# Attention scores computed for two heads at once on the two row halves of the array, in three products of 64 rows

## The chip, the cores and the metric

The kernel runs on one core of a Trainium2 chip. The metric is the device time of one execution in microseconds; lower is better. It is taken several times, and the median counts. Beside the timed runs, one execution is recorded by the hardware profiler, and every row below comes from such a record.

## The reference

The reference is a block of two layers over 512 latent tokens and 256 context tokens of 1024 features. Layer 0 is windowed attention with 16 query heads of 64 features, two key heads and a sink logit for each head. Layer 1 is differential attention with 8 heads, each with two score maps of 64 features. After each attention comes a squared-ReLU MLP. In outline, cut to the scores:

```
# layer 0, per block of 128 queries; keys: the block and its neighbours, and 256 context keys
s_lat = einsum('bqhgd,bkhd->bhgqk', qblk, kblk) * scale      # masked outside the window
s_ctx = einsum('bqhgd,bchd->bhgqc', qblk, kc) * scale
p     = softmax_with_sink(concatenate([s_lat, s_ctx]), sink)
o     = p[latent] @ v + p[context] @ vc
# context queries see the 256 context keys alone

# layer 1, per block of 128 queries; keys: all 768 tokens
s = einsum('bqhtd,bkhtd->bhtqk', qblk, keys) * scale          # t = 0, 1
p = softmax(s);  a = p[:, :, 0] - lam * p[:, :, 1]
o = a @ v_all
```

Everything is in float32.

## The kernel before, in words

**Products in parts.** A float32 operand is split into a high part of type float32r and the rest as a low part, both in SBUF (`split`, L505; `wsplit`, L301). A product of two such operands is three products, high by high, high by low and low by high (`mm3`, L324 to L327). The scores use another form. The head size is 64, so a score product has 64 rows to sum over, and the array has 128. In layer 1 the transposed keys of one map (`kS`) hold the high part in rows 0 to 63 and the low part in rows 64 to 127. The queries are written twice before they are transposed, so `qT` holds the high part in both halves, and, beside it, the low part in both halves. Two products of 128 rows then give all four combinations of parts. In layer 0 the roles are turned: the transposed keys are doubled (`kT[:, kvh, hl]`), and the queries of a head hold the high part above the low part.

**Layer 0.** `group(n, tb, qd)` (L1302) handles one block of 128 queries and four heads: 24 groups, 16 for the four latent blocks and 8 for the two context blocks. For each head it takes a score slot and an `e` tile, issues two products with the latent keys of the window (L1322; 256 or 384 columns) and two with the context keys (L1326; 256 columns). VectorE adds the mask, takes the minimum and copies the scores out of PSUM into `e`, and that frees the score slot. ScalarE takes the exponential, GpSimd scales, TensorE transposes (`pT_ps`, L1377) and multiplies by the values (`o_ps`, L1359, in two column halves of 64).

**Layer 1.** `post1` (L1612) takes a block of a head's projections, applies the rotation, splits keys and queries (`sk`, `sq`) and transposes them: two transposes for the keys (L1642) and, for latent blocks, four for the queries (L1657). `scores1` (L1726) goes over four query blocks, and for each over the two maps `tt`: one score slot, four products of 384 columns (L1738), a minimum on VectorE, an exponential on ScalarE straight from PSUM. The exponential frees the slot. `att1` (L1768) transposes the result and multiplies by the values.

**Score slots.** PSUM has two score tiles of 1024 columns, two banks each (tag "S", `psS`), counted by `sS = Slots(fl, 2)`. `ok` says that at least one is free, `spare` (L197) that at least two are. The `e` tiles are counted in the same way: `eS` in layer 0 (six at first, more later), `eS1` in layer 1 (five).

**What sets the order.** TensorE's order is written out by hand: a planner (`Flow`) runs the jobs as Python generators. A job yields a condition, and the planner takes the first job, by priority, whose condition holds at its own modelled time. The model charges `mm(n)` for a product and `dve`, `act`, `pool2` for the other engines. TensorE then works strictly in the order that came out. In layer 0 the groups have priorities 0.5 to 0.73; the query projections `proj` have 2 and the output projection 3. In layer 1 `att1` has 0.2, `scores1` 0.5, `post1` 1, `proj1` 2 and the output projection `out1` 3. The other engines' order follows the dependencies of the program.

Of the kernel before, what the change touches and what calls it, by code (L numbers as in the profile page):

```python
# [13 lines left out]
F32 = mybir.dt.float32  # L14
# [16 lines left out]
GRID_W = 64  # L31
ROPE_BASE = 10000.0
# [202 lines left out]
def hybrid_block(ctx: ExitStack, tc: tile.TileContext, t: dict, out: bass.AP):  # L235
# [834 lines left out]
    with tc.tile_pool(name="qpool", bufs=6, side="right") as qpool, \  # L1070
# [164 lines left out]
        def q_post(half, tb, pt, p, give):  # L1235
# [9 lines left out]
            stg = stg.rearrange("p (g u d) -> p g u d", g=8, u=2)  # L1245
            _, r = split(512, r, qr, stg[:, :, 0], stg[:, :, 1])
# [7 lines left out]
            for j in range(8):  # L1254
                nc.tensor.transpose(out=pq.bitcast(F32R)[:, j * P:(j + 1) * P], in_=stg[:, j], identity=identr)
# [3 lines left out]
            qT[(half, tb)] = qt.rearrange("p (h t) -> p h t", h=8)  # L1259
# [42 lines left out]
        def group(n, tb, qd):  # L1302
# [9 lines left out]
            for j in range(4):  # L1312
                yield [sS.ok, eS.ok]
                hd_ = qd * 4 + j
                q_ = qT[(kvh, tb)][:, hd_ % 8]
                esl.append(eS.take())
                e = etile(esl[-1])
                sp = psS("s_ps")
                slot = sS.take()
                for hl in range(2):  # L1320
                    if nl:
                        nc.tensor.matmul(out=sp[:, 512 - nl:512], lhsT=q_,  # L1322
                                         rhs=kT[:, kvh, hl, lat[0] * P:lat[0] * P + nl],
                                         start=(hl == 0), stop=(hl == 1))
                for hl in range(2):
                    nc.tensor.matmul(out=sp[:, 512:512 + CTX], lhsT=q_,  # L1326
                                     rhs=kT[:, kvh, hl, SEQ:TOK], start=(hl == 0), stop=(hl == 1))
                p = fl.pe(2 * mm(CTX) + (2 * mm(nl) if nl else 0))
                eo, si = e[:, 0:W_], sp[:, 512 - nl:512 + CTX]
                if tb == NXB - 1:  # L1330
                    mk = mask.rearrange("p (a b) k -> p a b k", a=2)[:, :, 0:2]
                    eo = eo.rearrange("p (a b k) -> p a b k", a=2, b=2)
                    si = si.rearrange("p (a b k) -> p a b k", a=2, b=2)
                else:
                    mk = mask.rearrange("p a b -> p (a b)")[:, 5 * P - W_:5 * P]
                nm = small.tile([P, 1], F32, name="nm", tag="nm")
                d = dv(W_ + 70, [p], nc.vector.tensor_tensor_reduce, out=eo, in0=si, in1=mk, scale=1.0,
                       scalar=nsink[:, hd_:hd_ + 1], op0=ALU.add, op1=ALU.min, accum_out=nm)
                sS.give(slot, d)

                d = [d, ac(1, [], nc.scalar.copy, out=e[:, W_:W_ + 1], in_=nsink[:, hd_:hd_ + 1])]
                sm = small.tile([P, 1], F32, name="sm", tag="sm")
                a = ac(W_ + 200, d, nc.scalar.activation, out=e[:, 0:W_ + 1], in_=e[:, 0:W_ + 1], func=AF.Exp,
                       scale=-1.0, bias=nm, accum_out=sm)
                d = dv(8, [a], nc.vector.reciprocal, out=sm, in_=sm)
                ready.append(gp(W_ * 0.0019 + 0.1, [d], nc.gpsimd.tensor_tensor, lat=ELAT, out=e[:, 0:W_], in0=e[:, 0:W_],
                                in1=sm.broadcast_to([P, W_]), op=ALU.mult))
                es.append(e)
                yield
# [241 lines left out]
    with tc.tile_pool(name="attn1", bufs=1, reuse_waits="tile") as pool:  # L1591
# [20 lines left out]
        def post1(hd_, tb, pt, p, give, R):  # L1612
# [39 lines left out]
            if isx:  # L1652
# [3 lines left out]
                for i in range(4):  # L1656
                    nc.tensor.transpose(out=pq.bitcast(F32R)[:, i * P:(i + 1) * P], in_=sq[:, i // 2, i % 2], identity=identr)  # L1657
# [419 lines left out]
```

## Time and profile before

| what | time |
|---|---|
| median of three runs | 1665.86 us |
| lowest and highest | 1658.1 and 1666.66 us |
| the profiled execution | 1660.59 us |
| its span, first to last instruction | 1658.5 us |
| its mean granted TensorE clock | 0.983 |
| scores of layer 0 on TensorE, first to last start | 74.8 to 298.4 us |
| scores of layer 1 on TensorE, first to last start | 929.8 to 1235.4 us |

In the rows of the profile, PE is TensorE's products and PEld its weight loads, DVE is VectorE, ACT is ScalarE and POOL is GpSimd. A row of the timeline gives a start, a length and how many like instructions were merged. The length of a product includes its way through the array, so successive products overlap in the rows; what a product costs when TensorE is the limit is the distance from its start to the next start. A form such as 128*64 128x256 says that the weights have 128 rows and 64 columns and that 256 columns are streamed.

### The profile page before, as it was taken

To read this page: it belongs to the slowest core of one execution; us is meant where nothing else is said; L and a number is where in the kernel's file an instruction comes from. 1 tells how busy PE (TensorE), PEld (TensorE's weight loads), DVE (VectorE), ACT (ScalarE), POOL (GpSimd) and SP (SyncE) were. 2 spreads that over 40 slices of the span, in tenths; PEclk is the share of its full clock that TensorE was granted. 3 is DMA by queue.
4 is the path that set the end of the run, shared out by engine and by line. 5 is a ranking of instruction groups with operands and counts; after the bars stand their busy time and mean duration, and the time that the engine had idled before them with its cause. 6 is when DMAs were issued, how large, how long until landed. Compare 5 with 4: busy or idle time off the path is not lost.

```text
span 1658.5 us, 25161 instructions
## 1 busy us (share of the span) xinstructions
PE 1572.0 (95%) x9465; PEld 1384.3 (83%) x9465; DVE 1139.5 (69%) x2199; ACT 790.7 (48%) x1683; POOL 440.4 (27%) x369
## 2 busy tenths in 40 slices
PE   7899999989999999999997999999989799999987
PEld 5788777789888998989986999899878789999986
DVE  4655676699776689766466677777765866666677
ACT  3465676364343334335416555555552745555450
POOL 1333444106111121211191222220100112222363
PEclk9999999999999999999998999999999899999998
DMA  9111550533454434443323122211132333333321
GB/s 372 43 52 33 179 178 26 197 128 128 143 162 150 140 103 163 153 141 115 125 71 111 52 70 64 74 46 39 48 115 90 102 115 102 102 102 102 102 77 51
DMA packets 66434, 181.17 MB, mean 109 GB/s; under 512 B 7368, under 2 KB 13320, under 8 KB 66312
## 3 DMA queue, kind: packets, MB, share of 16 engines
q1 hardware_dynamic: 66312, 179.56, 32.1%
q8 instruction: 74, 1.21, 0.3%
q14 instruction: 48, 0.39, 0.1%
HBM read 168.49 MB, written 11.04 MB: 108 GB/s over the span
## 4 chain that ended last, share of the span: by engine, by line
PE 53%; DVE 17%; DMA 11%; issue 7%; ACT 6%; POOL 5%; SPq 0%; DVEq 0%; POOLq 0%; ACTq 0%
PE y_ps L325 6%; PE y_ps L327 6%; PE y_ps L326 6%; DMA w_raw<-in_w_adaT 6%; PE h_ps L325 4%; PE h_ps L326 4%; PE h_ps L327 4%; DVE w_raw L260 2%; DVE w_l L314 2%; PE o_ps L1359 2%; PE pT_ps L1377 2%; PE qkv_ps L325 2%; PE qkv_ps L326 2%; PE qkv_ps L327 2%; PE s_ps L1738 2%
## 5 line engine op out<-in xcount | busy, mean ns | idle before, releaser
L325 PE MATMUL y_ps<-w_h,hid 128*128 128x512 f32 (+1 forms) x648 | 255.5, 394 | 3.3 <-ACT hid L264 2.4
L327 PE MATMUL y_ps<-w_h,hid 128*128 128x512 f32 (+1 forms) x648 | 254.6, 393 | 2.6 <-DVE hid L260 2.6
L326 PE MATMUL y_ps<-w_l,hid 128*128 128x512 f32 (+1 forms) x648 | 254.7, 393 | 0.5 <-DVE w_l L314 0.5
L314 DVE TENSOR_TENSOR w_l<-w_raw,w_h 128x1024 fp32r<-128x1024 f32 (+1 forms) x133 | 158.1, 1199 | 61.7 <-ACT w_h L264 58.5
L264 ACT CAST w_h<-w_raw 128x1024 fp32r<-128x1024 f32 (+1 forms) x133 | 131.2, 1001 | 113.8 <-PE y_ps L327 65.2
L268 POOL TENSOR_TENSOR w_sum<-w_raw 128x512 f32<-128x512 f32 x26 | 55.2, 2121 | 420.7 <-DMA w_raw<-in_w 272.7
L327 PEld LDWEIGHTS y_ps<-w_h,hid 128*128 128x128 f32 x648 | 123.6, 191 | 29.9 <-DVE hid L260 4.1
L325 PEld LDWEIGHTS y_ps<-w_h,hid 128*128 128x128 f32 x648 | 123.7, 191 | 27.1 <-ACT hid L264 3.5
L326 PEld LDWEIGHTS y_ps<-w_l,hid 128*128 128x128 f32 x648 | 123.8, 191 | 22.7 <-DVE w_l L314 0.9
L264 ACT CAST w_half<-w_raw 128x512 fp32r<-128x512 f32 x130 | 80.2, 620 | 114.1 <-PE h_ps L327 69.2
L325 PE MATMUL qkv_ps<-w_h,hx 128*128 128x384 f32 (+1 forms) x384 | 127.9, 333 | 3.4 <-ACT w_h L264 3.3
L260 DVE TENSOR_TENSOR w_half<-w_raw,w_half 128x512 fp32r<-128x512 f32 x130 | 105.9, 822 | 29.8 <-ACT w_half L264 28.1
L326 PE MATMUL qkv_ps<-w_l,hx 128*128 128x384 f32 (+1 forms) x384 | 123.1, 321 | 1.7 <-DVE w_l L314 1.7
L327 PE MATMUL qkv_ps<-w_h,hx 128*128 128x384 f32 (+1 forms) x384 | 122.8, 320 | 0.0
L268 POOL TENSOR_TENSOR e<-e,sm 128x512 f32<-128x512 f32 (+2 forms) x96 | 92.6, 977 | 109.6 <-DVE sm L260 91.0
L260 DVE CUSTOM_DVE_ANT_0 w_raw<-w_raw,cB 128x512 f32<-128x512 f32 x112 | 82.9, 768 | 42.0 <-DMA w_raw<-in_w_adaT 41.8
L260 DVE TENSOR_TENSOR fx<-y_ps,fx 128x512 f32<-128x512 f32 x110 | 75.3, 687 | 39.2 <-PE y_ps L327 38.4
L264 ACT ACTIVATE relu<-relu 128x384 f32<-128x384 f32 (+3 forms) x104 | 69.7, 672 | 50.1 <-DVE relu L260 49.0
L268 POOL TENSOR_TENSOR rope<-rope,rope 128x256 f32<-128x256 f32 (+1 forms) x40 | 33.8, 844 | 221.6 <-DVE rope L260 175.2
L264 ACT COPY relu<-h_ps 128x384 f32<-128x384 f32 (+1 forms) x78 | 32.9, 422 | 119.5 <-PE h_ps L327 113.0
L264 ACT ACTIVATE e<-e,nm 128x513 f32<-128x513 f32 (+2 forms) x96 | 65.9, 688 | 33.1 <-DVE nm L260 26.4
L325 PEld LDWEIGHTS qkv_ps<-w_h,hx 128*128 128x128 f32 x384 | 72.9, 190 | 5.3 <-ACT w_h L264 3.8
(267 smaller groups left out, 4329.6 us busy)
## 6 DMA issues: line engine op xcount, KB each, us to landing
w_raw<-in_w SPq DMA_DIRECT2D x128, 512.0 KB, 3.5
w_raw<-in_w_adaT SPq DMA_DIRECT2D x56, 512.0 KB, 3.8
w_raw<-in_w_ada SPq DMA_DIRECT2D x24, 512.0 KB, 4.3
w_raw<-in_b_w SPq DMA_DIRECT2D x32, 384.0 KB, 3.8
raw<-in_w_ada SPq DMA_DIRECT2D x16, 512.0 KB, 9.6
w_raw<-in_a_wq SPq DMA_DIRECT2D x8, 512.0 KB, 8.0
w_raw<-in_a_wo SPq DMA_DIRECT2D x8, 512.0 KB, 4.3
w_raw<-in_b_wo SPq DMA_DIRECT2D x8, 512.0 KB, 4.5
```

The costliest lines, as they stand in the source:

```text
L260: fn(**kw)
L264: fn(**kw)
L268: fn(**kw)
L314: last["split"] = nc.vector.tensor_tensor(**kw)
L325: nc.tensor.matmul(out=o, lhsT=lh, rhs=rh, start=start, stop=False, **kw)
L326: nc.tensor.matmul(out=o, lhsT=lh, rhs=rl, start=False, stop=False, **kw)
L327: last["pe"] = nc.tensor.matmul(out=o, lhsT=ll, rhs=rh, start=False, stop=stop, **kw)
L1359: nc.tensor.matmul(out=po[odd * HD:odd * HD + HD, 0:256], lhsT=vv[:, kb, kvh], rhs=pt_[:, odd * 256:odd * 256 + 256], start=(i == 0), stop ...
L1377: nc.tensor.transpose(out=pp[:, c * P:(c + 1) * P], in_=es[j][:, i * P:(i + 1) * P], identity=ident)
L1738: nc.tensor.matmul(out=sp[:, c * 512:c * 512 + 384], lhsT=qTt[:, tt, hl, qb * P:(qb + 1) * P], rhs=kS[:, tt, c * 384:c * 384 + 384], start ...
```

## The change

Two heads of layer 0, or the two maps of a head in layer 1, are computed together. One lies in rows 0 to 63 of the transposed tiles, the other in rows 64 to 127. For each stretch of keys there are three passes (`PASSES`): high by high, high by low, low by high. Low by low is no longer computed. In each pass one product of 64 rows is issued for the first head and one for the second, into two different score tiles. So a pair has six products where two heads had four.

- `q_post` (layer 0) stores the split queries as high part, then low part, and transposes two heads at a time: still eight transposes a block.
- `post1` (layer 1) no longer doubles the queries: the split works on half the elements, there are two transposes a block instead of four, and `qT1` is half as large. `sk` is laid out by part first, so that `kS[:, part]` holds the two maps in its two row halves.
- Both score loops take two score slots and two `e` tiles at once; they wait for `spare` where they waited for `ok`. The softmax of both heads is issued after all products of the pair.
- The planner is told three products of each length for a pair.

The core of the diff (the softmax lines of layer 0 are only indented further):

```diff
+PASSES = ((0, 0), (0, 1), (1, 0))
...
-            stg = stg.rearrange("p (g u d) -> p g u d", g=8, u=2)
-            _, r = split(512, r, qr, stg[:, :, 0], stg[:, :, 1])
+            sh, sl = [stg[:, x:x + 512].rearrange("p (g d) -> p g d", d=HD) for x in (0, 512)]
+            _, r = split(512, r, qr, sh, sl)
...
-            qT[(half, tb)] = qt.rearrange("p (h t) -> p h t", h=8)
+            qT[(half, tb)] = qt.rearrange("p (h j t) -> p h j t", h=2, j=4)
...
-            for j in range(4):
-                yield [sS.ok, eS.ok]
...
-                for hl in range(2):
-                    if nl:
-                        nc.tensor.matmul(out=sp[:, 512 - nl:512], lhsT=q_,
-                                         rhs=kT[:, kvh, hl, lat[0] * P:lat[0] * P + nl],
-                                         start=(hl == 0), stop=(hl == 1))
-                for hl in range(2):
-                    nc.tensor.matmul(out=sp[:, 512:512 + CTX], lhsT=q_,
-                                     rhs=kT[:, kvh, hl, SEQ:TOK], start=(hl == 0), stop=(hl == 1))
-                p = fl.pe(2 * mm(CTX) + (2 * mm(nl) if nl else 0))
...
+            for j in range(2):
+                yield [sS.spare, eS.spare]
+                q_ = qT[(kvh, tb)][:, :, (qd % 2) * 2 + j]
+                two = []
+                for i in range(2):
+                    esl.append(eS.take())
+                    two.append((qd * 4 + 2 * j + i, etile(esl[-1]), psS("s_ps"), sS.take()))
+                for o, k0, n in ([(512 - nl, lat[0] * P, nl)] if nl else []) + [(512, SEQ, CTX)]:
+                    for ph, pk in PASSES:
+                        for i in range(2):
+                            r_ = slice(i * HD, i * HD + HD)
+                            nc.tensor.matmul(out=two[i][2][:, o:o + n], lhsT=q_[r_, ph], rhs=kT[r_, kvh, pk, k0:k0 + n],
+                                             start=(ph == 0 and pk == 0), stop=(ph == 1))
+                p = fl.pe(3 * mm(CTX) + (3 * mm(nl) if nl else 0))
+                for hd_, e, sp, slot in two:
...
-            _, d1 = split(P, r, kr, sk[:, :, 0], sk[:, :, 1], [rsk.get()])
+            _, d1 = split(P, r, kr, sk[:, 0], sk[:, 1], [rsk.get()])
             if isx:
-                sq = pool.tile([P, 2, 2, 2, HD], F32R, name="sq", tag="sq", bufs=SB)
-                q_ = qk[:, 0:2].unsqueeze(2).broadcast_to([P, 2, 2, HD])
-                _, d2 = split(256, r, q_, sq[:, :, 0], sq[:, :, 1], [rsq.get()])
+                sq = pool.tile([P, 2, 2, HD], F32R, name="sq", tag="sq", bufs=SB)
+                _, d2 = split(P, r, qk[:, 0:2], sq[:, 0], sq[:, 1], [rsq.get()])
...
-                for i in range(4):
-                    nc.tensor.transpose(out=pq.bitcast(F32R)[:, i * P:(i + 1) * P], in_=sq[:, i // 2, i % 2], identity=identr)
-                p = fl.pe(4 * mm(P))
+                for i in range(2):
+                    nc.tensor.transpose(out=pq.bitcast(F32R)[:, i * P:(i + 1) * P], in_=sq[:, i], identity=identr)
+                p = fl.pe(2 * mm(P))
...
-                for tt in range(2):
-                    yield [sS.ok, eS1.ok]
...
-                    for c in range(2):
-                        for hl in range(2):
-                            nc.tensor.matmul(out=sp[:, c * 512:c * 512 + 384], lhsT=qTt[:, tt, hl, qb * P:(qb + 1) * P],
-                                             rhs=kS[:, tt, c * 384:c * 384 + 384], start=(hl == 0), stop=(hl == 1))
...
+                yield [sS.spare, eS1.spare]
+                two = [(psS("s_ps"), sS.take(), eS1.take()) for _ in range(2)]
+                for c in range(2):
+                    for ph, pk in PASSES:
+                        for tt in range(2):
+                            r_ = slice(tt * HD, tt * HD + HD)
+                            nc.tensor.matmul(out=two[tt][0][:, c * 512:c * 512 + 384],
+                                             lhsT=qTt[r_, ph, qb * P:(qb + 1) * P], rhs=kS[r_, pk, c * 384:c * 384 + 384],
+                                             start=(ph == 0 and pk == 0), stop=(ph == 1))
+                p = fl.pe(6 * mm(384))
```

More of the change, by code (lines that the diff above doesn't have):

```diff
@@ L1254, in q_post @@
             for j in range(8):
-                nc.tensor.transpose(out=pq.bitcast(F32R)[:, j * P:(j + 1) * P], in_=stg[:, j], identity=identr)
+                nc.tensor.transpose(out=pq.bitcast(F32R)[:, j * P:(j + 1) * P], in_=stg[:, j * P:(j + 1) * P], identity=identr)
             p = fl.pe(8 * mm(128))
@@ new lines, in group @@
+            for j in range(2):
[13 more added lines that the diff above has]
+                for hd_, e, sp, slot in two:
+                    eo, si = e[:, 0:W_], sp[:, 512 - nl:512 + CTX]
+                    if tb == NXB - 1:
+                        mk = mask.rearrange("p (a b) k -> p a b k", a=2)[:, :, 0:2]
+                        eo = eo.rearrange("p (a b k) -> p a b k", a=2, b=2)
+                        si = si.rearrange("p (a b k) -> p a b k", a=2, b=2)
+                    else:
+                        mk = mask.rearrange("p a b -> p (a b)")[:, 5 * P - W_:5 * P]
+                    nm = small.tile([P, 1], F32, name="nm", tag="nm")
+                    d = dv(W_ + 70, [p], nc.vector.tensor_tensor_reduce, out=eo, in0=si, in1=mk, scale=1.0,
+                           scalar=nsink[:, hd_:hd_ + 1], op0=ALU.add, op1=ALU.min, accum_out=nm)
+                    sS.give(slot, d)
+                    d = [d, ac(1, [], nc.scalar.copy, out=e[:, W_:W_ + 1], in_=nsink[:, hd_:hd_ + 1])]
+                    sm = small.tile([P, 1], F32, name="sm", tag="sm")
+                    a = ac(W_ + 200, d, nc.scalar.activation, out=e[:, 0:W_ + 1], in_=e[:, 0:W_ + 1], func=AF.Exp,
+                           scale=-1.0, bias=nm, accum_out=sm)
+                    d = dv(8, [a], nc.vector.reciprocal, out=sm, in_=sm)
+                    ready.append(gp(W_ * 0.0019 + 0.1, [d], nc.gpsimd.tensor_tensor, lat=ELAT, out=e[:, 0:W_],
+                                    in0=e[:, 0:W_], in1=sm.broadcast_to([P, W_]), op=ALU.mult))
+                    es.append(e)
@@ L1671, in proj1 @@
                     "kS": pool.tile([P, 2, TOK], F32R, name="kS1", tag="kS1", bufs=2),
-                    "qT": pool.tile([P, 2, 2, SEQ], F32R, name="qT1", tag="qT1", bufs=2),
+                    "qT": pool.tile([P, 2, SEQ], F32R, name="qT1", tag="qT1", bufs=2),
                     "vt": pool.tile([P, NTB, 2, P], F32R, name="vt1", tag="vt1", bufs=2),
@@ L1730, in scores1 @@
                 em = []
-                for tt in range(2):
-                    yield [sS.ok, eS1.ok]
-                    ei = eS1.take()
-                    sp = psS("s_ps")
-                    slot = sS.take()
-                    for c in range(2):
-                        for hl in range(2):
-                            nc.tensor.matmul(out=sp[:, c * 512:c * 512 + 384], lhsT=qTt[:, tt, hl, qb * P:(qb + 1) * P],
-                                             rhs=kS[:, tt, c * 384:c * 384 + 384], start=(hl == 0), stop=(hl == 1))
+                yield [sS.spare, eS1.spare]
[8 more added lines that the diff above has]
+                p = fl.pe(6 * mm(384))
+                for tt, (sp, slot, ei) in enumerate(two):
                     sv = sp.rearrange("p (b t) -> p b t", b=2)[:, :, 0:384]
-                    p = fl.pe(4 * mm(384))
                     nm = small.tile([P, 1], F32, name="nm", tag="nm")
@@ L1752, in scores1 @@
                     em.append((e, sm, ei, a))
-                    yield
+                yield
                 (e0, s0, i0, _), (e1, s1, i1, _) = em
```

29 lines of the change are left out of this document (2 added, 27 removed).

## The prediction

> **What bounds the kernel now.** I read the page's busy lines first.
>
> ```profile
> span 1658.5 us, 25161 instructions
> PE 1572.0 (95%) x9465; PEld 1384.3 (83%) x9465; DVE 1139.5 (69%) x2199; ACT 790.7 (48%) x1683; POOL 440.4 (27%) x369
> ```
>
> TensorE is busy nearly throughout, but a busy share includes overlapped latency, so I then asked for the busy times in the stretches in which scores run (layer 0, layer 1, and the end of layer 1).
>
> ```profile
> 70.00:300.00 230.00, 224.20 (x1640) 176.24 (x1638) 148.26 (x429) 142.82 (x400) 100.30 (x101) 1.00 0.25 87
> 925.00:1220.00 295.00, 283.28 (x1945) 269.12 (x1945) 210.61 (x447) 164.71 (x385) 58.26 (x70) 0.99 0.18 56
> 1220.00:1250.00 30.00, 24.60 (x140) 20.88 (x140) 18.56 (x30) 13.14 (x26) 1.04 (x1) 1.00 0.42 155
> ```
>
> The columns are length, then PE, PEld, DVE, ACT and POOL busy. TensorE is busy 97% of layer 0's stretch and 96% of layer 1's, with VectorE at 65% and 71%: there a saved microsecond of TensorE is a saved microsecond of span. Only the last 30 us, at 82%, are paced by something else. So the change is worth what it does to the spacing of TensorE's instructions.
>
> **The products.** The groups of the scores, by shape:
>
> ```profile
> L1738 PE MATMUL s_ps<-kS,qT 128*128 128x384 f32 x256 | 56.9, 351 | 1.9 <-ACT e L264 1.8
> L1326 PE MATMUL s_ps<-kT,qT 128*128 128x256 f32 x192 | 37.1, 288 | 0.0
> L1322 PE MATMUL s_ps<-kT,qT 128*128 128x384 f32 x64 | 18.4, 368 | 0.1
> L1322 PE MATMUL s_ps<-kT,qT 128*128 128x256 f32 x64 | 14.2, 304 | 2.8 <-DVE nm L260 2.8
> ```
>
> The means there are latencies; the cost is the distance between starts, which the timeline of TensorE gives. Layer 1, around one score batch:
>
> ```profile
> 1011.65 0.34 PE L327 MATMUL qkv_ps<-w_h,hx 128*128 128x384 f32 x1
> 1011.92 0.50 PE L1874 MATMUL rms_bc<-rh,id 2*128 2x512 f32 x1
> 1012.26 0.39 PE L1876 MATMUL rms_bc<-rl,id 2*128 2x512 f32 x1
> ...
> 1012.72 0.39 PE L1876 MATMUL rms_bc<-rl,id 2*128 2x512 f32 x1
> 1013.03 1.66 PE L1738 MATMUL s_ps<-kS,qT 128*128 128x384 f32 x8
> 1014.53 0.34 PE L325 MATMUL qkv_ps<-w_h,hx 128*128 128x384 f32 x1
> ...
> 1018.70 0.88 PE L1738 MATMUL s_ps<-kS,qT 128*128 128x384 f32 x4
> 1019.41 0.34 PE L325 MATMUL qkv_ps<-w_h,hx 128*128 128x384 f32 x1
> ```
>
> The four scores from 1018.70 to the next projection take 0.71 us, so 0.175 each with rounding. A score batch inside projections costs nothing beyond its products. For 256 columns:
>
> ```profile
> 1003.03 0.28 PE L327 MATMUL qkv_ps<-w_h,hx 128*128 128x256 f32 x1
> 1003.24 0.43 PE L1835 MATMUL rms_ps<-osq,c_selT 128*32 128x128 f32 x8
> 1003.60 0.39 PE L325 MATMUL qkv_ps<-w_h,hx 128*128 128x256 f32 x1
> 1003.82 0.29 PE L326 MATMUL qkv_ps<-w_l,hx 128*128 128x256 f32 x1
> ...
> 1004.18 0.29 PE L326 MATMUL qkv_ps<-w_l,hx 128*128 128x256 f32 x1
> ...
> 1004.65 0.28 PE L327 MATMUL qkv_ps<-w_h,hx 128*128 128x256 f32 x1
> ```
>
> The last two rows are four starts apart: 0.47 / 4 = 0.118. (I take 0.175 and 0.118 throughout.) The scores cost 256 x 0.175 + 64 x 0.175 + 256 x 0.118 = 44.8 + 11.2 + 30.2 = 86.2 us.
>
> The change makes three pairs of 64-row products out of every four 128-row ones. If the two of a pair run together, and a pair costs one slot, that is a quarter off: **-21.6 us** (11.2 in layer 1, 10.4 in layer 0). If they run one behind the other it is half on, +43 us. No row shows two row halves at work. The nearest are products on parts of the array's columns: the eight 32-column records at 1003.24 take 0.36 us until the next product, change of shape included, where eight full-width transposes (the x8 row below) span 1.03. Parts of the array do overlap, so I take one slot a pair and keep +43 for the upper end.
>
> **The queries of layer 1.** L1657 goes from four transposes a block to two; with 8 heads and 4 blocks, 64 go. The rows for four of them:
>
> ```profile
> 1000.44 0.68 PE L1657 MATMUL qT_ps<-identr,sq 128*128 128x128 f32 x4
> 1000.96 0.35 PE L325 MATMUL qkv_ps<-w_h,hx 128*128 128x256 f32 x1
> ...
> 1023.71 0.46 PE L1657 MATMUL qT_ps<-identr,sq 128*128 128x128 f32 x4
> 1024.00 0.41 PE L325 MATMUL qkv_ps<-w_h,hx 128*128 128x384 f32 x1
> ...
> 1241.76 1.03 PE L1804 MATMUL pT_ps<-identr,e 128*128 128x128 f32 x8
> ```
>
> Between 0.07 (0.29 / 4) and 0.13 (0.52 / 4) each; the first row's time holds a gap, so I take 0.08: **-5.1 us** (-4.5 to -8.3). The split of the queries and ScalarE's copy of the transposed ones (the row below) lose half their elements. They run beside TensorE's projections, which hide them; I cost them at nothing, and uncovered the copy alone could give 32 x 0.3 = 10 us.
>
> ```profile
> L264 ACT ACTIVATE qT<-qT_ps 128x512 fp32r<-128x512 f32 x32 | 19.1, 598 | 4.4 <-PE qT_ps L1657 4.0
> ```
>
> Layer 0's copies keep their sizes (512 elements, eight transposes); only the order inside the tile moves. No DMA and no queue is touched.
>
> **The change of shape.** This is the term against. The 2-row products at 1011.92 stand between full products. Going in, the start is 0.27 after a product worth 0.175 and the second start 0.34 after the first, where 0.23 is usual: 0.10 + 0.11. Coming out, 0.31 in place of 0.23, and the eight scores take 1.50 in place of 1.40: 0.08 + 0.10. So about **0.20 us a crossing**, 0.4 in and out. The 32-column products show the same: 0.21 in place of 0.118 at 1003.24, and 0.22 in place of 0.118 at 1003.82. What it looks like is a drained array whose first weight load is exposed. A 64-row batch is a third shape, not in this trace; I take 0.20 from the nearest row, the 2-row one, with 0 (no drain) as the lower end.
>
> Here a rule speaks against the change: the Trainium skill, "TensorEngine Tiling (Array Packing)", section "Key Properties", says that a change of tiling mode, not of tile, drains the engine. The trace agrees for 2-row and 32-column shapes (0.4 us in and out); by the rule a 64-row batch pays too, without it the crossings below are free.
>
> How many crossings: 48 pairs in layer 0 (96 heads) and 32 in layer 1 (8 heads, 4 blocks). They stay separate batches, since a pair waits for its slots. That makes 96 and 64 edges. Where an edge touches products that are column-tiled already, a crossing was paid before:
>
> ```profile
> 101.55 1.95 PE L1359 MATMUL o_ps<-pT,v 128*64 128x256 f32 x16
> 103.42 0.62 PE L1322 MATMUL s_ps<-kT,qT 128*128 128x384 f32 x2
> ```
>
> Along the timeline, 24 of layer 0's edges now touch o_ps or ada_ps (these rows are the first such pair), and 3 of layer 1's touch rms_bc. Kept so: 96 - 24 + 64 - 3 = 133 new crossings x 0.20 = **+26.6 us** (0 to 32). This all but cancels -21.6 - 5.1 = -26.7.
>
> **The added wait.** A pair waits for both score slots (and two e tiles) instead of one. Everything behind it in TensorE's written order waits too, though the planner places other work while its model has the slots taken. In the middle of both layers such work exists. The last head of layer 1 has little:
>
> ```profile
> 1226.38 1.85 PE L1738 MATMUL s_ps<-kS,qT 128*128 128x384 f32 x8 [0.32 <-ACT e L264]
> 1227.37 0.96 DVE L260 TENSOR_REDUCE nm<-s_ps 128x1 f32<-128x768 f32 x1 [1.21 <-PE s_ps L1738]
> 1228.37 0.90 ACT L264 ACTIVATE e<-s_ps,nm 128x768 f32<-128x768 f32 x1 [1.16 <-DVE nm L260]
> 1229.16 0.19 ACT L264 ACTIVATION_READ_ACCUMULATOR e<-s_ps,nm 128x1 f32 x1
> 1229.41 1.91 PE L1738 MATMUL s_ps<-kS,qT 128*128 128x384 f32 x8 [1.19 <-ACT e L264]
> 1234.09 1.66 PE L1738 MATMUL s_ps<-kS,qT 128*128 128x384 f32 x8
> ```
>
> Now a pair starts every 3.0 us there (1226.38 to 1229.41). With both slots needed it is pair 1.05, exposed load 0.1, two reduces 1.9, exp and its read 1.1: 4.15. Two of the three intervals are that short (the third, 4.7 us, is already longer): 2 x 1.1 = **+2.2 us**. Without other work in the middle, the same 1.1 us would fall on many of the 80 pairs, at most 88 us; -3 is possible, since fewer batches mean fewer waits.
>
> **The sum.** -21.6 - 5.1 + 26.6 + 2.2 = +2.1 us. The profiled execution took 1660.59 us (span 1658.5 and 2.1 around it), so 1662.7 on its own scale. The median of the three runs, 1665.86, lies 5.3 above that execution: **1668 us**, which is no change, as 0.5% (8.3 us) is what a measurement of this kernel can tell.
>
> **The rivals.**
> - *No drain between 64-row and full shapes.* For it: no row shows a 64-row product, and score batches of today mix freely with projections. Against: the 2-row rows. Then 2.1 - 26.6 = -24.5: 1641.
> - *Crossings half hidden*: batches that start where TensorE waits anyway, or beside o_ps. For it: the waits of 0.32 and 1.19 above, and the 24 edges. Against: stretches at 97%. Then -13.3 + 2.1 = -11.2: 1655.
> - *The two weight loads of a pair go one behind the other* (the other side, slower). The place is every pair after its first. The two rows below show loads starting 0.11 apart after a change of shape, so two would need 0.21 or more.
>
> ```profile
> 1008.37 0.19 PEld L325 LDWEIGHTS qkv_ps<-w_h,hx 128*128 128x128 f32 x1
> 1008.48 0.19 PEld L326 LDWEIGHTS qkv_ps<-w_l,hx 128*128 128x128 f32 x1
> 1003.24 0.16 PEld L1835 LDWEIGHTS rms_ps<-osq,c_selT 128*32 128x32 f32 x8
> ```
>
>   All 432 pair slots (240 of 384 columns, 192 of 256) would cost 0.215: 92.9 in place of the forecast's 64.6, so +28.3 + 2.1 = +30: 1696. It is slower by 0.5% from a mean pair slot 14 ns over a single product's (6.2 / 432). Against it: the eight loads of the last row fit into 0.16 us. Pairs that overlap only in part for another reason land here as well. The Trainium skill, "TensorE: Matmul & The Clock Gate", section "Measured speedup vs the span model", gives 3.07 times for four row tiles, which no run here shows; as an estimate from it a pair would cost 1.3 slots, and the time would be near 1688.
> - *The two slots starve the score chain* in the context part of layer 0 too: sixteen pairs at 1 us each, +16 + 2.1: 1684. Against: the planner has output products to put between.
> - *The pairs don't run together at all*: 432 x 2 products cost 43 + 21.6 us more: 1733. I give it little.
>
> **How the numbers follow.** Forecast 0.42, no drain 0.13, half hidden 0.15, loads in turn (with the few hundredths of no overlap) 0.15, starving 0.15. Around the forecast's own 1668, 1658 to 1678, a new written order may move the waits by some us either way: of its 0.42, 0.03 are faster by over 0.5% (below 1657.5), 0.30 within, 0.09 slower (above 1674.2). No drain gives 0.13 faster; half hidden 0.09 faster and 0.06 within; loads 0.15 slower; starving 0.13 slower and 0.02 within. Sums: faster 0.25, same 0.38, slower 0.37. The range runs from between the first two rivals to the loads in turn: 1644 to 1694.
>
> **What would show it.** In the changed profile the two products of a pair start within some ns of each other, and pairs follow at 0.175 and 0.118; 0.21 for both would be the loads. The first pair after full products starts about 0.1 late, and the second pair about 0.1 later than its slot; the product after a batch shows the same. L1657 counts 64, the score products 768. The last head's pairs stand 4 us apart. The forecast is wrong if the crossings are missing, or if the 97% of layer 0's stretch falls.

## The result, and the profile after

The changed kernel takes **1673.89 us** (median of five runs, 1671.25 to 1677.99). The kernel before, timed beside it, takes 1660.6 us (1657.57 to 1666.66). The ratio is 1.0083 with an interval of 1.0062 to 1.0105: slower by some 13 us. The forecast was +2.1 us. The two profiled executions differ by 13.3 us of span, and the first of these lines is the span after. The lines are from the page of the changed kernel.

```profile
span 1671.8 us, 25615 instructions
PE 1573.6 (94%) x9689; PEld 1360.3 (81%) x9689; DVE 1139.1 (68%) x2199; ACT 776.5 (46%) x1683; POOL 438.7 (26%) x369
```

TensorE is busy 1.6 us longer than before and idle 11.7 us longer. So the loss appears as waiting, as far as busy time can tell the two apart. The mean granted clock of the span is 0.983 in both. The next view has the busy times in the three stretches for which the prediction showed them (length, then PE, PEld, DVE, ACT and POOL busy, and the granted clock).

```profile
70.00:300.00 230.00, 218.46 (x1721) 161.12 (x1720) 146.25 (x396) 132.79 (x370) 96.81 (x93) 0.99 0.26 87
925.00:1220.00 295.00, 277.67 (x1988) 252.19 (x1986) 206.94 (x452) 152.42 (x392) 57.73 (x71) 0.99 0.18 55
1220.00:1250.00 30.00, 25.36 (x167) 20.68 (x165) 19.89 (x33) 14.81 (x31) 1.04 (x1) 0.89 0.28 94
```

TensorE's share falls from 97% to 95% in layer 0's stretch and from 96% to 94% in layer 1's. In the last row the granted clock is 0.89 where it was 1.00.

To see where the 13 us lie I cut the span at four products that every version has: the first `q_ps`, the last `o_ps` of layer 0, the first `qkv_ps`, the last `rms_bc`, and from there to the last product.

| stretch | before | after | difference |
|---|---|---|---|
| layer 0: first `q_ps` to last `o_ps` | 279.66 | 292.76 | +13.1 |
| from there to the first `qkv_ps` (MLP of layer 0) | 591.71 | 586.69 | -5.0 |
| layer 1: to the last `rms_bc` | 365.02 | 370.51 | +5.5 |
| rest: to the last product | 385.97 | 385.64 | -0.3 |

Layer 0's +13.1 us is as much as the whole difference; the -5.0 and +5.5 of the next two stretches cancel. The forecast's terms divide into +4.0 us for layer 0 (products -10.4, crossings +14.4) and -1.9 us for layer 1 (products -11.2, transposes -5.1, crossings +12.2, wait +2.2).

The pairs themselves behave as forecast. The timeline of TensorE around one pair of layer 1 and one of layer 0 (start, length, instructions merged):

```profile
981.29 0.34 PE L327 MATMUL qkv_ps<-w_l,hx 128*128 128x384 f32 x1
981.46 0.34 PE L328 MATMUL qkv_ps<-w_h,hx 128*128 128x384 f32 x1
981.73 1.33 PE L1735 MATMUL s_ps<-kS,qT 64*128 64x384 f32 x12
983.00 0.44 PE L326 MATMUL qkv_ps<-w_h,hx 128*128 128x384 f32 x1
983.27 0.34 PE L327 MATMUL qkv_ps<-w_l,hx 128*128 128x384 f32 x1
983.45 0.34 PE L328 MATMUL qkv_ps<-w_h,hx 128*128 128x384 f32 x1
...
288.42 0.62 PE L1324 MATMUL s_ps<-kT,qT 64*128 64x256 f32 x6
288.96 0.50 PE L326 MATMUL y_ps<-w_h,hx 128*128 128x512 f32 x1
289.30 0.40 PE L327 MATMUL y_ps<-w_l,hx 128*128 128x512 f32 x1
289.54 0.39 PE L328 MATMUL y_ps<-w_h,hx 128*128 128x512 f32 x1
```

From 981.46 to 983.27 there are eight starts: one projection, six pairs, one projection. Eight slots of 0.175 are 1.40 us; the rows give 1.81. So a pair costs one slot, and the batch costs 0.41 us for going in and coming out. Single starts inside the row of twelve: the two products of a pair start 3 to 17 ns apart, and the pairs start at 981.733, 982.011, 982.189, 982.366, 982.541 and 982.714. The first pair is 0.095 us late, the second 0.10, and the projection behind the batch and the one after it 0.09 and 0.10 each. In layer 0's batch the three pairs start at 288.415, 288.641 and 288.756: 0.226 from the first to the second and 0.115 from the second to the third.

### The profile page after: what moved, and what is told of

Read it like the earlier page. It is cut to its first block, busy times and chain, and to the rows that moved or that the text cites. A ratio compares the mean times of both kernels' runs of the same rounds, so it can differ in the third digit from the quotient of the medians.

```text
span 1671.8 us, 25615 instructions
## 1 busy us (share of the span) xinstructions
PE 1573.6 (94%) x9689; PEld 1360.3 (81%) x9689; DVE 1139.1 (68%) x2199; ACT 776.5 (46%) x1683; POOL 438.7 (26%) x369
## 4 chain that ended last, share of the span: by engine, by line
PE 57%; DVE 18%; issue 7%; ACT 7%; DMA 6%; POOL 5%; SPq 0%; DVEq 0%; POOLq 0%; ACTq 0%
PE y_ps L326 8%; PE y_ps L328 7%; PE y_ps L327 7%; PE h_ps L326 5%; PE h_ps L327 5%; PE h_ps L328 5%; ACT e L265 3%; DMA w_raw<-in_w_adaT 3%; PE qkv_ps L326 2%; PE o_ps L1358 2%; PE qkv_ps L327 2%; PE qkv_ps L328 2%; PE s_ps L1324 2%; PE pT_ps L1376 2%; DVE e L261 2%
## 5 line engine op out<-in xcount | busy, mean ns | idle before, releaser
L326 PEld LDWEIGHTS qkv_ps<-w_h,hx 128*128 128x128 f32 x384 | 72.3, 188 | 11.7 <-issue 4.9
```

What stands on the lines that cost most here:

```text
L326: nc.tensor.matmul(out=o, lhsT=lh, rhs=rh, start=start, stop=False, **kw)
```

## The experiments

Each kernel is told with its ratio to the kernel before, timed on the same chip, with a 95% interval in brackets. This table has the same stretches as above, each from one profiled execution; "told" is what the planner is told of a pair's products, in full products a stretch of keys, where it isn't what is issued.

| kernel | layer 0 | MLP 0 | layer 1 | rest |
|---|---|---|---|---|
| before | 279.66 | 591.71 | 365.02 | 385.97 |
| e10_before_lat (before, a lateness told) | 280.68 | 591.28 | 372.00 | 383.28 |
| e8_before34 (before, told 3) | 283.58 | 592.32 | 382.17 | 386.01 |
| e12_before5 (before, told 5) | 279.02 | 586.84 | 403.94 | 384.35 |
| e3_gate | 285.74 | 592.89 | 384.65 | 386.09 |
| e4_full | 279.65 | 588.57 | 365.92 | 384.72 |
| after | 292.76 | 586.69 | 370.51 | 385.64 |
| e1_layer0 | 292.33 | 588.04 | 366.96 | 386.54 |
| e2_layer1 | 280.41 | 589.80 | 372.94 | 385.29 |
| e7_cross | 294.46 | 587.38 | 374.90 | 385.19 |
| e9_l1_lat (e2, a lateness told) | 279.28 | 588.58 | 372.94 | 383.75 |
| e6_l1_told (e2, told 0.4 us more) | 280.06 | 588.93 | 384.47 | 384.94 |
| e5_told (after, told 0.4 us more) | 294.04 | 588.06 | 383.93 | 385.14 |
| e11_after4 (after, told 4) | 294.04 | 587.67 | 387.13 | 385.98 |

### One layer at a time: e1_layer0 and e2_layer1

`e1_layer0` is the changed kernel with layer 1 as it was; `e2_layer1` is the changed kernel with layer 0 as it was.

```diff
 # e1_layer0, in layer 1
-                yield [sS.spare, eS1.spare]
...
-                p = fl.pe(6 * mm(384))
...
+                for tt in range(2):
+                    yield [sS.ok, eS1.ok]
...
+                    p = fl.pe(4 * mm(384))
...
 # e2_layer1, in layer 0
-            for j in range(2):
-                yield [sS.spare, eS.spare]
+            for j in range(4):
+                yield [sS.ok, eS.ok]
...
```

> Pairs in layer 0 only; layer 1 is that of the kernel before. Theory 'crossings and waits' (each change of shape costs 0.2 us, so layer 0 gives back all it saves; on top come waits of a new written order): the last o_ps of layer 0 ends 13 us later than before, as in the changed kernel, and the whole is 8 to 13 us longer than the kernel before. Rival 'layer 1 is what costs' (its gate on two slots): under 4 us longer.

> Pairs and undoubled queries in layer 1 only; layer 0 is that of the kernel before. Theory 'crossings and waits': products, transposes and crossings of layer 1 come to -4 us, its waits to +8, so 2 to 7 us longer than the kernel before. Rival 'layer 0 is all of it': 3 to 5 us shorter.

Measured: e1 1675.85 us, 1.0076 [1.005, 1.0103]; e2 1662.49 us, 1.0001 [0.9984, 1.0017]. Layer 0's half of the change alone costs what the whole costs; layer 1's half alone makes no difference that can be told, which is between its two expectations. In the table layer 0 takes 292.3 to 294.5 us in all five kernels that have its pairs, and 279.0 to 283.6 in the seven that have its single products. So the 13 us are of layer 0, and no accident of one written order.

### Gate, products and crossings: e3_gate and e4_full

`e3_gate` issues the full-row products of before, four for two heads, but takes two slots at once as the change does. `e4_full` keeps the changed kernel's slots and written order, and issues three full-row products a stretch of keys in place of three pairs. It leaves out part of the scores' terms; what it tells is the time of the change without its crossings.

```diff
 # e3_gate: against before (layer 1 likewise, 8 * mm(384))
-            for j in range(4):
-                yield [sS.ok, eS.ok]
+            for j in range(2):
+                yield [sS.spare, eS.spare]
...
+                p = fl.pe(4 * mm(CTX) + (4 * mm(nl) if nl else 0))
...
 # e4_full: against the changed kernel (layer 1 likewise)
-                    for ph, pk in PASSES:
-                        for i in range(2):
-                            r_ = slice(i * HD, i * HD + HD)
-                            nc.tensor.matmul(out=two[i][2][:, o:o + n], lhsT=q_[r_, ph], rhs=kT[r_, kvh, pk, k0:k0 + n],
-                                             start=(ph == 0 and pk == 0), stop=(ph == 1))
+                    for ph, pk, i in ((0, 0, 0), (0, 1, 0), (1, 0, 1)):
+                        nc.tensor.matmul(out=two[i][2][:, o:o + n], lhsT=q_[:, ph], rhs=kT[:, kvh, pk, k0:k0 + n],
+                                         start=(pk == 0), stop=(ph == 1 or pk == 1))
```

> The kernel before with its own full-row products and doubled operands, but both heads of a pair are taken together: wait for two slots and two e tiles, all eight products, then both softmaxes. No crossings, no saving. Theory 'crossings and waits': the gate alone brings its waits, 5 to 15 us longer than the kernel before. Rival 'the gate costs nothing, crossings are dearer than 0.2 us': within 3 us of the kernel before.

> The changed kernel with its order and gate, but for each pair and stretch of keys three full-row products in place of six half-row ones (two into the first head's score tile, one into the second's). It leaves out or mixes parts of the scores, so the output is not the reference's; the count of product slots is the same and no change of shape is left. Theory 'crossings and waits': 133 crossings of 0.2 us go, 22 to 28 us shorter than the changed kernel, so 9 to 15 us shorter than the kernel before. Rival 'crossings are hidden in waits anyway': under 10 us shorter than the changed kernel.

Measured: e3 1680.84 us, 1.011 [1.0077, 1.0142]; e4 1659.16 us, 0.9987 [0.9971, 1.0003]. e3 is some 18 us above the kernel before, where 5 to 15 were expected. e4 is some 16 us below the changed kernel, between the theory's 22 to 28 and the rival's 10, and only 2 below the kernel before, where 9 to 15 were expected. The windows over layer 0, first of the kernel before, then of e3_gate, e4_full and the changed kernel:

```profile
25.00:304.00 279.00, 269.78 (x1960) 211.37 (x1958) 178.19 (x498) 164.36 (x444) 112.25 (x114) 1.00 0.29 103
```

```profile
25.00:310.00 285.00, 273.35 (x1960) 211.57 (x1958) 182.21 (x498) 162.33 (x444) 114.66 (x114) 1.00 0.30 101
```

```profile
25.00:305.00 280.00, 265.48 (x1892) 202.45 (x1886) 181.15 (x498) 163.16 (x445) 114.00 (x114) 0.99 0.30 103
```

```profile
25.00:317.00 292.00, 276.01 (x2118) 204.29 (x2116) 183.59 (x498) 162.35 (x444) 114.56 (x114) 0.99 0.28 98
```

TensorE stands idle 9.2 us before, 11.7 in e3, 14.5 in e4 and 16.0 after. So e4 shows what became of the saved products. By the distance from each score batch's start to the next product's, scores cost 39.2 us in e4's layer 0 and 50.9 before: 11.7 saved. The stretch is 279.65 against 279.66: nothing saved. The gain is gone elsewhere, above all around `pT_ps` (47.4 against 39.0 us by the same measure), and TensorE's idle time is 5.3 us longer. A smaller part is clock: 3.4 us of e4's stretch, and of the changed kernel's, run at a granted clock of 0.50, which is worth at most 1.7 us; before has none there. The gate alone, in e3, makes layer 0 longer by 6.1 us, or by 2.2 against the slowest of the seven kernels with single products there.

From e4 to the changed kernel the written order stays and only the shape of the products changes: +13.1 us in layer 0, where I forecast 14.4 for 72 new crossings, and +4.6 in layer 1, where I forecast 12.2. In layer 0 the crossings cost almost what they were priced at, though TensorE idles there. In layer 1 some 7.6 us of them don't show. Part of that is waits that were there already (idle time falls by 3.3 us from e4 to the changed kernel), and part may be clock: e4 spends 19.8 us of layer 1 at a clock of 0.50 and the changed kernel 13.7, an estimate of 3 us.

e3's layer 1 is another matter: 384.65 against 365.02, 19.6 us for a gate. Its profiled execution was 6.5 us over its median, which is part of that; the next runs show that the order alone can do as much, and a table further down that most of it stands in a lower granted clock.

### One more crossing: e7_cross

Layer 1's batch of twelve is parted by one full-row product, whose result the second half's first product overwrites. That adds 32 such products and 64 crossings and nothing else; the written order stays.

```diff
                 for c in range(2):
+                    if c:
+                        nc.tensor.matmul(out=two[0][0][:, 512:640], lhsT=qTt[:, 0, qb * P:(qb + 1) * P], rhs=kS[:, 0, 0:P],
+                                         start=True, stop=True)
```

> The changed kernel with one more full-row product of 128 columns between the two halves of each layer 1 pair (its result is overwritten): two more changes of shape in each of 32 batches. Theory 'a crossing costs 0.2 us of TensorE': in the trace each such batch is 0.45 us longer (0.4 and 0.06 for the product), 14 us in all, of which the waits beside them take back up to half: 7 to 14 us longer than the changed kernel. Rival 'crossings are cheap and the gate does it all': under 3 us longer.

Measured: 1679.68 us, 1.0118 [1.0075, 1.0161], some 6 us above the changed kernel, though the intervals of the two ratios overlap; it lies between the two expectations. The windows over layer 1 for the score tile alone, after and then e7_cross:

```profile
896.00:1281.00 385.00, 44.63 (x384) 33.26 (x384) 59.27 (x64) 63.13 (x128) 0.98 0.21 68
```

```profile
896.00:1281.00 385.00, 58.71 (x416) 37.32 (x416) 59.32 (x64) 63.00 (x128) 0.98 0.21 67
```

The scores take 14.1 us more: 0.44 for each of 32 insertions, of which some 0.06 is the product of 128 columns itself (0.118 for 256, halved). That leaves 0.19 a crossing, as priced. But layer 1 is longer by only 4.4 us. The waits show where the rest went. After, in layer 1 (us in total, times, longest):

```profile
PE o_ps L1775 <- DVE pT L261: 9.3, 7, 1.7
PE s_ps L1735 <- ACT e L265: 3.5, 4, 2.1
...
PE kT_ps L1640 <- DVE sk L261: 2.2, 7, 0.8
```

And in e7_cross:

```profile
PE o_ps L1778 <- DVE pT L261: 3.5, 7, 0.8
PE s_ps L1738 <- ACT e L265: 3.4, 4, 2.1
```

The wait of the output products for `pT` gives back 5.8 us, in the same seven places. TensorE arrives later at a point where it had waited anyway. The kernel before hasn't got this wait, though another order of the same single products has (e12_before5, below). Of the kernel before, the list of waits in layer 1 begins so:

```profile
PE kT_ps L1642 <- DVE sk L260: 7.8, 6, 2.3
...
PE s_ps L1738 <- ACT e L264: 1.8, 3, 1.2
```

The timeline of the changed kernel ahead of one such wait, VectorE, ScalarE and TensorE:

```profile
949.14 0.95 DVE L261 TENSOR_REDUCE nm<-s_ps 128x1 f32<-128x768 f32 x1
...
950.87 0.95 DVE L261 TENSOR_REDUCE nm<-s_ps 128x1 f32<-128x768 f32 x1
...
951.42 0.58 ACT L265 CAST pT<-pT_ps 128x512 fp32r<-128x512 f32 x1
...
952.03 0.69 DVE L261 TENSOR_TENSOR pT<-pT_ps,pT 128x512 fp32r<-128x512 f32 x1 [0.20 <-ACT pT L265]
...
952.77 0.50 PE L1775 MATMUL o_ps<-pT,vt 128*128 128x256 f32 x2 [0.67 <-DVE pT L261]
```

Both reduces of a pair now stand close together in VectorE's queue, and the copies of `pT` of the head before come behind them. One wait (`kT_ps` for `sk`) has become another.

### Is it the order? e8_before34, e9_l1_lat and e10_before_lat

Since the planner writes another order when a charge changes, these runs change what it is told and nothing else. `e8_before34` is the kernel before with three quarters of the score charge, which is what the change tells. `e9_l1_lat` is e2_layer1 with the split of `pT` in layer 1 told 1.4 us late, so that the planner should put other work ahead of the new wait; `e10_before_lat` tells the kernel before the same.

```diff
 # e8_before34 (layer 1: 3 * mm(384))
-                p = fl.pe(2 * mm(CTX) + (2 * mm(nl) if nl else 0))
+                p = fl.pe(1.5 * mm(CTX) + (1.5 * mm(nl) if nl else 0))
...
 # e9_l1_lat and e10_before_lat: the split of pT in att1
-                    _, r = split(512, p, pp, pt_[:, 0], pt_[:, 1], lat=XLAT)
+                    _, r = split(512, p, pp, pt_[:, 0], pt_[:, 1], lat=1.4)
```

> The kernel before with nothing changed but the planner's charge for the score products, three quarters of it as in the changed kernel: another written order with the same work and no gate. Theory 'the gate costs, not just any new order': within 5 us of the kernel before. Rival 'any new order costs as much': over 8 us longer.

> Layer 1 alone changed, as in the run with pairs in layer 1 only, and the planner is told that the split of the transposed weights of layer 1 is done 1.4 us after its model says so (before: 0.2), so that the products with the values are placed later. Theory 'the two reduces of a pair stand in VectorE's queue before that split and the products with the values wait': the seven waits of o_ps for pT, 9 us, go, and the kernel is 3 to 9 us shorter than the kernel before. Rival 'the wait only moves': within 3 us of the kernel before.

> The kernel before with the same 1.4 us told to the planner and nothing else. Theory: it has no such waits of o_ps for pT, so it gains nothing: within 4 us of the kernel before. Rival 'the order told is better in itself': 3 us shorter or more.

Measured: e8 1682.15 us, 1.0119 [1.0074, 1.0165]; e9 1662.72 us, 1.0009 [0.9991, 1.0027]; e10 1668.41 us, 1.0033 [1.0007, 1.0058]. In e8 and e9 the rival came out, and e10 is some 5 us longer where at most 4 were expected (its interval reaches from 1 to 10). The same instructions in another order cost e8 1.2%, 17 us of it in layer 1. The waits of e8_before34 there:

```profile
PE kT_ps L1642 <- DVE sk L260: 13.5, 9, 2.3
PE s_ps L1738 <- ACT e L264: 4.6, 7, 1.2
```

So e3's loss in layer 1 can't be put down to its gate. In e9 the wait for `pT` falls from 9.2 us (e2) to 6.6, and layer 1 takes 372.94 in both: that wait looks like a place where lateness shows, and not like its source.

### The crossing told to the planner, and other orders: e5_told, e6_l1_told, e11_after4, e12_before5

If the planner knew of the 0.4 us a batch, its model would be nearer to the chip. `e5_told` adds that to the changed kernel, `e6_l1_told` to e2_layer1. `e11_after4` tells the changed kernel four products a pair, as before's two heads together; `e12_before5` tells the kernel before five quarters.

```diff
 # e5_told, both layers (layer 1: 6 * mm(384) + 0.4); e6_l1_told, layer 1 alone
-                p = fl.pe(3 * mm(CTX) + (3 * mm(nl) if nl else 0))
+                p = fl.pe(3 * mm(CTX) + (3 * mm(nl) if nl else 0) + 0.4)
...
 # e11_after4 (layer 1: 8 * mm(384))
+                p = fl.pe(4 * mm(CTX) + (4 * mm(nl) if nl else 0))
...
 # e12_before5 (layer 1: 5 * mm(384))
+                p = fl.pe(2.5 * mm(CTX) + (2.5 * mm(nl) if nl else 0))
```

> The changed kernel, with the planner told 0.4 us more for each pair, which is what the two crossings cost in the trace. Same work, another written order. Theory 'the changed kernel's extra time over the sum is its order, and orders differ by about 10 us either way': anywhere from 12 us shorter to 10 us longer than the changed kernel, and not the same. Rival 'the loss sits in the crossings, not in the order': within 3 us of the changed kernel.

> Layer 1 alone changed (that run was level with the kernel before), with the planner told 0.4 us more for each pair. By TensorE's own work layer 1 gains 4 us; if the waits fall back to those of the kernel before, 3 to 5 us shorter than it. If the order decides: anywhere within 10 us of it.

> The changed kernel, with the planner told four products a pair and stretch in place of three, as for the kernel before. Theory of the order: again another time, from 12 us shorter to 10 us longer than the changed kernel. Rival 'crossings': within 3 us of it.

> The kernel before, with the planner told five quarters of its charge for score products (three quarters gave 1.2% more time). Theory of the order: the kernel before has a lucky order and any other costs, 3 to 18 us longer. Rival 'a lower charge is what hurts': within 3 us or shorter.

Measured: e5 1689.47 us, 1.0192 [1.0161, 1.0222]; e6 1676.19 us, 1.0108 [1.0077, 1.0139]; e11 1693.39 us, 1.0214 [1.0187, 1.0241]; e12 1699.28 us, 1.024 [1.0206, 1.0274]. All are slower than the kernel they start from, by some 18 us (e5, e6), 22 (e11) and 40 (e12), which is more than any of the expectations allowed, and nearly all of the loss is in layer 1, which takes 384 to 404 us. The waits of e12_before5 in layer 1:

```profile
PE kT_ps L1642 <- DVE sk L260: 26.4, 16, 3.6
PE o_ps L1776 <- DVE pT L260: 6.5, 5, 1.9
```

What follows for layer 1: the kernel before takes 365.0, 372.0, 382.2 and 403.9 us there for the same work in four orders, and with pairs it takes 370.5 to 387.1 in six kernels. At a charge of three products the pairs are 12 us faster (370.5 against 382.2), at four 22 us slower (387.1 against 365.0). The effect of the pairs in layer 1 is smaller than that of the order, and its sign stays open.

How an order costs that much in layer 1 shows in the granted clock. In e3_gate TensorE waits 2.32 us for `sk`; behind that wait come 10.2 us at a clock of 0.50, in which eight score products take 2.93 us where they took 1.66 before (two rows of its timeline, then two windows):

```profile
1018.60 0.49 PE L1638 MATMUL kT_ps<-identr,sk 128*128 128x128 f32 x2 [2.32 <-DVE sk L260]
...
1023.07 2.93 PE L1732 MATMUL s_ps<-kS,qT 128*128 128x384 f32 x8
```

```profile
1018.30:1028.50 10.20, 9.90 (x29) 8.62 (x30) 5.73 (x8) 4.01 (x7) 0.00 (x0) 0.50 0.42 148
1028.60:1031.00 2.40, 2.40 (x15) 2.40 (x15) 0.48 (x3) 0.48 (x3) 0.00 (x0) 1.00 0.00 0
```

The next table has, for layer 1 of each profiled execution, TensorE's idle time and the time at a clock of 0.50. TensorE is busy for nearly all of such a time, so about half of it is lost: an estimate. The last column is what is left of layer 1 without the idle time and this half.

| kernel | layer 1 | idle | at clock 0.50 | left |
|---|---|---|---|---|
| before | 365.0 | 18.8 | 9.0 | 341.7 |
| e10_before_lat | 372.0 | 20.6 | 13.7 | 344.6 |
| e8_before34 | 382.2 | 26.2 | 29.5 | 341.2 |
| e12_before5 | 403.9 | 39.1 | 44.4 | 342.6 |
| e3_gate | 384.6 | 24.2 | 40.0 | 340.4 |
| e4_full | 365.9 | 27.8 | 19.8 | 328.2 |
| after | 370.5 | 24.5 | 13.7 | 339.2 |
| e2_layer1 | 372.9 | 23.8 | 23.9 | 337.2 |
| e6_l1_told | 384.5 | 29.1 | 34.1 | 338.3 |
| e5_told | 383.9 | 28.9 | 34.1 | 338.0 |
| e11_after4 | 387.1 | 32.7 | 20.5 | 344.2 |

What is left differs by 4 us among the five kernels with all the single products, whose layer 1 differs by 39. So an order costs by its waits and, about as much, by the lower clock: of e12's 39 us, 20 are idle time and some 18 clock, and of e3's 19.6 some 15 are clock. The timed executions agree: (1 - clock) x span is on average 11 us more than before's in e3, 6 in e8, 18 in e12, 15 in e5, 12 in e6 and 7 in e11. The 13 us of the change itself are not of this kind: its five executions have clocks of 0.982 to 0.986, and the kernel before 0.978 to 0.988.

No kernel that computes all the scores was measurably faster than the one before; e2_layer1 and e9_l1_lat are level with it.

## Why the prediction was right or wrong

The time fell into the range (1644 to 1694), above the likeliest case: forecast +2.1 us, measured +13. It is slower by over 0.5%, which had a chance of 0.37. The range is wide, and that the time lies in it is partly luck: most of what the sum lacks is a wait in layer 0 that it put at nothing, and the 7.4 us by which layer 1 is above its own sum are mostly offset by -5.0 in a stretch that the forecast left out.

**The pair at one slot: right.** Pairs follow at 0.175 us (384 columns) and 0.115 (256). This rules out the rival of weight loads in turn, which needed 0.21, and that of no overlap. The Trainium skill, "TensorE: Matmul & The Clock Gate", section "Measured speedup vs the span model", gives 3.07 times for four row tiles, from which the prediction estimated 1.3 slots for a pair; the trace doesn't agree with that estimate and shows one slot, a factor of two for two row halves.

**The crossing at 0.20 us: right.** 0.41 us in and out of one batch against 0.40 forecast, 0.19 a crossing over e7's 64, and 13.1 us over layer 0 against 14.4. In the trace after, 31 of layer 0's 96 edges touch `o_ps` or `ada_ps`, and not 24, so 65 crossings are new and cost 0.20 each. The rival of no drain falls. The rule of the Trainium skill, "TensorEngine Tiling (Array Packing)", section "Key Properties", that a change of tiling mode drains the engine, agrees with the trace: 0.41 us for a batch of 64-row products.

**"There a saved microsecond of TensorE is a saved microsecond of span": wrong.** This step, drawn from shares of 97% and 96%, carried both gains of the sum. e4_full has all of the gains (21.6 + 5.1 us by the forecast) without one crossing between halves and full rows, and is 2 us from the kernel before. TensorE is busy less there (338.1 us of layer 1 against 346.2), but waits longer and runs longer at the lower clock. Since e4 also takes two slots at once and has another order, it doesn't tell whether one of these would have spared the gain.

**"In the middle of both layers such work exists": wrong for layer 0.** I costed the wait for two slots there at nothing. The gate alone cost 6.1 us in layer 0 (e3), and where products were saved as well, nothing was left of the 10.4 (e4: layer 0 level with before). How much of this is the gate and how much the other order that comes with it, the runs don't part. The new waits after, in layer 0:

```profile
PE ada_t L392 <- ACT ada_rows L265: 4.0, 3, 1.9
PE qT_ps L1256 <- DVE nm L261: 3.4, 2, 2.3
PE s_ps L1324 <- DVE nm L261: 2.0, 5, 0.8
```

And the same three before:

```profile
PE s_ps L1322 <- DVE nm L260: 2.8, 3, 1.1
...
PE ada_t L391 <- ACT ada_rows L264: 0.5, 1, 0.5
...
PE qT_ps L1255 <- DVE nm L260: 0.2, 1, 0.2
```

The first two have grown from 0.5 and 0.2 us, and the third is no longer than it was. The queries' transposes use score slots too, and wait now behind the two minima of a pair. The rival that I gave this, starving at 1 us a pair in the context part, had the right place and sign and was too large (16 us); layer 0's own sum is short of the result by 9.1 us (+4.0 against +13.1), and 6.8 of that is idle time; up to 1.7 is the lower clock, which follows the wait of 2.3 for `qT_ps`. In e1_layer0, which has the same pairs at full clock, idle time is 7.8 us longer than before.

**Crossings half hidden: a partial truth.** In layer 0 they cost 13.1 of 14.4; in layer 1 4.6 of 12.2 (after against e4, of which some 3 may be clock), and e7's added 14.1 came out as 4.4. The rival put the waits in the wrong place: in e7 they hide crossings where TensorE meets another engine behind them, as `o_ps` with `pT`.

**The transposes and queries of layer 1.** The count is right, 64 (the row below, from L1655 after). Their gain, 5.1 us, was not seen by itself; with layer 1's products it is in e4, whose layer 1 is level with before because it idles 9.0 us longer and spends 10.8 us more at a clock of 0.50.

```profile
L1655 PE MATMUL qT_ps<-identr,sq x64: 221/250/328, 925.0 to 1223.6; 128*128 128x128 f32 x64
L1735 PE MATMUL s_ps<-kS,qT x384: 327/335/685, 936.6 to 1248.0; 64*128 64x384 f32 x192
L1324 PE MATMUL s_ps<-kT,qT x480: 272/279/443, 76.6 to 312.3; 64*128 64x256 f32 x128, 64*128 64x384 f32 x32
```

The last two rows are 864 score products; the 768 in the prediction was a slip, since its own 432 pairs make 864.

**The last head: right in kind.** +2.2 us forecast for pairs 4 us apart. The timeline after:

```profile
1235.54 0.44 PE L1735 MATMUL s_ps<-kS,qT 64*128 64x384 f32 x1 [0.50 <-ACT e L265]
1236.42 1.34 PE L1735 MATMUL s_ps<-kS,qT 64*128 64x384 f32 x11 [0.44 <-ACT e L265]
1237.79 1.82 DVE L261 TENSOR_REDUCE nm<-s_ps 128x1 f32<-128x768 f32 x2
...
1239.82 0.43 PE L1735 MATMUL s_ps<-kS,qT 64*128 64x384 f32 x1 [2.07 <-ACT e L265]
1240.70 2.28 PE L1735 MATMUL s_ps<-kS,qT 64*128 64x384 f32 x11 [0.45 <-ACT e L265]
```

The distance from 1235.54 to 1239.82 is 4.28 us (4.15 forecast). The rows also show that a pair doesn't wait whole: its first product starts when the first slot is free, and the second product 0.88 us later. From the first to the last score of this head it is 15.9 us where it was 12.3: +3.6. What I missed is the row of 2.28, below.

**"A new written order may move the waits by some us either way": mis-sized.** The same work in another order moved layer 1 by 7 to 39 us. This width, more than any term of the sum, decides layer 1, and about half of it is the lower clock behind longer waits, for which the sum has no term.

**Not forecast: MLP 0, -5.0 us.** No product there is changed. Kernels without pairs in layer 0 take 586.8 to 592.9 us in this stretch, so the kernel before is at its upper part; those with pairs take 586.7 to 588.1. Most of the 5 us is clock, by estimate: 25.1 us of the stretch run at 0.50 before and 17.1 after, and half of the difference is 4.0. Why the clock fell less often was not tried.

## What to carry to other kernels

Running two half-row products side by side halves their cost, but a batch of another shape costs 0.4 us to enter and leave here, so a batch has to save more than that: six pairs in place of eight products save two slots, 0.35 us. A busy share of 97% doesn't show that saved time shortens the span; where the order of an engine is fixed, a run that takes the work away (as e4_full) shows it, and it is best done first. Where a planner writes the order, a change of a few per cent has to be compared at several orders, since the order alone moved this kernel by up to 2.4%. In such a comparison the granted clock of each stretch belongs beside its time: waits of about 2 us cost this kernel about as much again in clock behind them.

## What the runs showed of the hardware that was not expected

In the last head of the changed kernel five of a batch's six pairs stand 0.32 us apart (single starts at 1241.195, 1241.515, 1241.835 and 1242.155) where 0.175 is usual: the row of 2.28 us for eleven products above, against 1.34 for the batch before. The windows there:

```profile
1236.00:1240.00 4.00, 1.52 (x12) 1.19 (x12) 3.14 (x5) 1.59 (x5) 0.00 (x0) 1.00 0.45 181
1240.00:1243.00 3.00, 2.55 (x13) 1.86 (x14) 1.69 (x4) 0.65 (x2) 0.00 (x0) 0.52 0.00 0
1243.00:1250.00 7.00, 6.96 (x42) 6.18 (x42) 5.69 (x10) 3.33 (x7) 0.00 (x0) 0.72 0.09 27
```

The granted clock (the column after the POOL count) is 1.00 while TensorE is busy 1.52 of 4 us, then 0.52 in the 3 us behind the wait of 2.07, and 0.72 for 7 us more: it is 0.50 from 1240.1 to 1246.9 us. The Trainium skill, "TensorE: Matmul & The Clock Gate", section "Part 1: The HAM clock gate", has the clock at half rate after an idle window of about 3.4 us; the trace agrees on the half, and shows it after a shorter wait, with two of 0.5 us and 0.44 us and busy time between. Before, where the longest wait of the head is 1.92 us (the row below), it stays at 1.00. The same batch shows the same slow pairs in e2_layer1, e7_cross, e9_l1_lat and e11_after4, each behind a wait of 2.06 to 2.09 us, and in e1_layer0, whose longest wait there is 1.94, it doesn't. So the waits for two slots in this head appear to cost clock as well: 3 x 0.48 + 7 x 0.28 = 3.4 us of TensorE's time at full speed, an estimate of which only a part can lie on the path, since layer 1's end, from the last score to the last `rms_bc`, is longer by 1.0 us (26.6 against 25.5).

```profile
1233.35 0.99 PE L1804 MATMUL pT_ps<-identr,e 128*128 128x128 f32 x7 [1.92 <-DVE e L260]
```

How often a wait is followed by the lower clock depends on its length, in layer 1 of all fourteen kernels (counted from 8 us after its start): of 19 waits of more than 2.2 us that began at full clock, 18 have the clock go to 0.50 before their end or within 3.6 us of it; of 22 between 1.9 and 2.2 us 16 have it, of 12 between 1.6 and 1.9 us 6, and of 66 between 1.0 and 1.6 us 3.
